# Order of casts, tiles and decay logs in the front of a hybrid attention block

## The chip, the core and the metric

One core of one Trainium2 chip runs the whole program. The metric is device time in microseconds (us), the median of several executions. The engines in the text: TensorE (PE, matmuls; PEld is its weight load), VectorE (DVE), ScalarE (ACT), GpSimd (POOL) and SyncE (SP, which here only issues DMAs). "PEq", "SPq" and the like are the engines' queues of issued work.

## What is computed

One layer of a streaming encoder for 512 frames of width 1024: RMSNorm, one wide projection `w_in`, three branches (gated linear attention, forgetting attention "Fox", cross attention into 256 memory tokens), their gated sum, an output projection, a squared-ReLU MLP and a last RMSNorm. What matters for the change:

```python
u = rmsnorm(h, g_mix[l])
proj = u @ w_in[l]
(gq, gk, gv, gg, ga, fq, fk, fv, ff, mq, gates) = split_cols(proj, PROJ_SIZES)

log_a = jax.nn.log_sigmoid(ga @ w_alpha_up[l] + b_alpha[l]) / GLA_TAU
...
log_f = jax.nn.log_sigmoid(ff + b_forget[l])
o_fox = forgetting_attention(fq, fk, fv, log_f)

mkv = rmsnorm(mem, g_mem[l]) @ w_mem_kv[l]
```

`ga` (16 columns) and `ff` (8 columns) are the low-rank input of the decay and the forget gate. Both go through a log-sigmoid: these are the decay logs. `rmsnorm(mem)` needs the sum of squares of each memory token.

## The kernel before

All matmul operands are kept as two parts, `hi` (the value cast to fp32r) and `lo` (the rest), and each product is three matmuls: hi by hi, hi by lo, lo by hi (`mm3`, L150 to L152). A weight chunk is 128 x 1024 (512 KB). It is loaded by SP into a ring of three buffers `raw` (or, for chunks 3, 4, 7 and 10 of the front, into a ring of two named `lead`), cast by ACT to `hi`, and subtracted by DVE to `lo`; `hi` and `lo` have rings of three. So a chunk's cast waits for its load and for the last matmul that read the buffer's older content, and a new load waits for the older chunk's subtraction.

Work on PE runs in the order in which the program traces it. On ACT, DVE, POOL and SP a planner orders instructions by a simulated time line: it takes what is ready in the simulation, earlier traced work first. Two things bind it. `in_order()` (L205) fixes the traced order on ACT, DVE and PE; the front stage from L348 on lies in it. `tc.issue_after(ins)` puts every instruction of its block that runs on the engine of `ins` behind `ins`.

The front: memory keys and values are projected from unnormalised memory tokens (chunks 0 to 7 of `FIRST_W`), while x is squared and its row scale is computed. The row scale is spread over partitions by eight small matmuls (`bcast_rows`, L241) and copied by ACT to `rxb` (L249). Then the eight tiles of x are handled one by one: `x_high(k)` (L412) scales tile k on DVE and casts it on ACT to `uhi`, `x_low(k)` (L416) subtracts on DVE to `ulo`. Between them stand the splits of weight chunks 7 (last memory values), the low-rank chunk (ACT cast L426, DVE subtraction L429), 9 (first Fox queries) and 10 (first Fox keys).

Behind it, the lead (L648 to L652): a low-rank projection (2 matmuls for each tile of x), the first pair's Fox queries (3 matmuls a tile) and keys (3 a tile) are traced as a staircase: low-rank tile s, queries tile s-1, keys tile s-2. `decay_logs()` (L478) multiplies the low-rank result by `wup` in four matmul pairs, each into its own PSUM bank, and takes Abs, Exp and Ln on ACT and minima and subtractions on DVE. The ring `pa` has four PSUM banks; the banks of the low-rank result, of the keys and of the four products follow each other in it. `fv = v_chunks(...)` is the projection of Fox's values: four chunks of eight units of three matmuls; a unit's number in `islice(fv, n)` counts such triples. `decay_sums()` (L490) multiplies the logs by triangular matrices, `decay_rows()` (L504) transposes the sums and writes them to DRAM. `mem_split()` (L627) squares the memory tokens (eight squares on ACT, seven adds on DVE into `memsum`), sums over partitions on PE (L231), and later scales and splits the memory's keys and values; its first part ends at `yield`.

In the profile L201 and L202 are the two halves of the helper `split`, L141 and L142 those of `split_w`, L297 and L303 those of `first_high` and `first_low`, L413 the scaling of x and L417 its low half, L463 and L464 the low-rank matmuls, L481 the four matmul pairs of the logs, L635 and L636 the squares and adds of the memory.

Of the kernel before, what the change touches and what calls it, by code (L numbers as in the profile page):

```python
# [13 lines left out]
AF = mybir.ActivationFunctionType  # L14
ALU = mybir.AluOpType
# [46 lines left out]
def hybrid_block(ctx, tc, chunks, wst, xT, memT, xN, cols, gffn, gfin, wup, cst, out):  # L62
# [214 lines left out]
    with pool("front") as fp:  # L277
        rxb = sg[3]
        xr = fp.tile([P, KT, S], F32, name="xr")
        FIRST_W = [chunks[j] for j in range(8)] + [("G",), ("T", "w_in", OFF["fq"]), ("T", "w_in", OFF["fk"])]  # L280
        raws, ready, loads = {}, {}, {}

        def first_load(i, n=1):
            late = i in (3, 4, 7, 10)
            raws[i] = (fp if late else wp).tile([P, 1024], F32, tag="lead" if late else "raw", name=nm("raw"),
                                                bufs=2 if late else 3)
            for j in range(n):
                sl = slice(j * 1024 // n, (j + 1) * 1024 // n)
                loads[i] = (nc.scalar if n > 1 and j < 3 else nc.sync).dma_start(raws[i][:, sl], wst[index[FIRST_W[i]]][:, sl]).ins
                if n > 1:  # L290
                    yield

        def first_high(i, n=1, j=0):
            if i not in ready:
                ready[i] = [wp.tile([P, 1024], F32R, tag=g, name=nm(g)) for g in ("hi", "lo")]
            sl = slice(j * 1024 // n, (j + 1) * 1024 // n)
            cast = nc.scalar.copy(ready[i][0][:, sl], raws[i][:, sl])  # L297
            if i > 4:
                next_sum(cast.ins)

        def first_low(i, n=1, j=0):
            sl = slice(j * 1024 // n, (j + 1) * 1024 // n)
            nc.vector.tensor_tensor(ready[i][1][:, sl], raws[i][:, sl], f(ready[i][0][:, sl]), op=ALU.subtract)  # L303

        def first_split(i, n=1, j=0):
            first_high(i, n, j)
            first_low(i, n, j)

        def first_w(i):
            run(first_load(i))  # L310
            first_split(i)

        get_plain = get_w

        def get_first(key):
            return ready[FIRST_W.index(key)]

        get_w = get_first
        mxh = fp.tile([P, KT, M], F32R, name="mxh")
        mxl = fp.tile([P, KT, M], F32R, name="mxl")  # L320
        xacc = dct[:, :S]
        warm = fp.tile([P, 1], F32, name="warm")
        nc.vector.memset(warm, 0.0)
        wz = fp.tile([P, 512], BF16, name="wz")
        nc.gpsimd.memset(wz, 0.0)
        ps = at_()
        for _ in range(12):
            nc.tensor.matmul(ps, wz[:, :P], wz, start=True, stop=True)

        kv = {}  # L330

        def mem_in(k):
            return sg[k // 2][:, k % 2 * M:k % 2 * M + M] if k < 6 else dct[:, 4 * S + (k - 6) * M:4 * S + (k - 5) * M]

        def mk_raw(h):
            return gkT[h // 2][:, (h % 2) * M:(h % 2) * M + M]

        def mk_proj(h):
            return gT(("T", "w_mem_kv", P * h), mxh, mxl, lambda ps: kv.update({h: ps}), n=M)

        def mk_take(h):
            nc.scalar.copy(mk_raw(h), kv[h][:, :M])

        def x_squares(*ks):
            for k in ks:
                sq_col(fp, xr, S, k, xacc, "x")

        with in_order():  # L348
            nc.scalar.activation(warm, warm, AF.Exp)
            nc.scalar.dma_start(cols_s, cols)  # L350
            quarters = first_load(0, 4)
            for j in range(4):
                to = sg[j] if j < 3 else dct[:, 4 * S:5 * S]
                nc.sync.dma_start(to.rearrange("p (k t) -> p k t", k=2), memT[:, 2 * j:2 * j + 2])
                next(quarters)

            def x_load(j):
                nc.sync.dma_start(xr[:, 2 * j:2 * j + 2], xT[:, 2 * j:2 * j + 2])

            run(first_load(1), first_load(2))  # L360
            x_load(0)
            run(first_load(3))
            for j in range(1, 4):
                x_load(j)
            nc.sync.dma_start(cst_s[:, :2 * P], cst[:, :2 * P])
            nc.sync.dma_start(cst_s[:, 5 * P:], cst[:, 5 * P:])
            run(first_load(4))
            for k in range(KT):
                m = mem_in(k)
                nc.scalar.mul(mxh[:, k, :], m, gmem[:, k:k + 1])  # L370
                nc.vector.scalar_tensor_tensor(mxl[:, k, :], m, gmem[:, k:k + 1], f(mxh[:, k, :]),
                                               op0=ALU.mult, op1=ALU.subtract)
                if k % 2 == 0:
                    first_split(0, 4, k // 2)
            first_split(1, 2, 0)
            first_split(1, 2, 1)
            first_split(2)
            x_squares(0, 1)
            run(mk_proj(0))
            first_split(3)  # L380
            x_squares(2, 3)
            run(mk_proj(1))
            x_squares(4, 5, 6, 7)
            run(mk_proj(2))
            mk_take(0)
            mk_take(1)
            first_split(4)
            run(mk_proj(3))
            rx = rms_cols(fp, xacc, S)
            first_w(5)  # L390
            mk_take(2)
            mk_take(3)
            mv = gN([("N", "w_mem_kv", 2 * j, 512) for j in range(4)], of(mxh, mxl), 2, mmt,
                    lambda t, ps: kv.update({("v", t): ps}))
            for i in (6, 7):
                run(first_load(i))
            g_raw = load_w(("G",))
            for i in (9, 10):
                run(first_load(i))
            run(islice(mv, 6))  # L400
            put = bcast_rows(fp, rx, S, rxb)
            next(put)
            first_high(6)
            run(put)
            first_low(6)
            run(islice(mv, 6))
            with tc.issue_after(loads[7]):
                nc.sync.dma_start(cst_s[:, 2 * P:5 * P], cst[:, 2 * P:5 * P])
                nc.sync.dma_start(wup_s, wup)
            ends = {}  # L410

            def x_high(k):  # L412
                nc.vector.scalar_tensor_tensor(xr[:, k, :], xr[:, k, :], gmix[:, k:k + 1], rxb, op0=ALU.mult, op1=ALU.mult)  # L413
                ends[0] = nc.scalar.copy(uhi[:, k, :], xr[:, k, :]).ins

            def x_low(k):  # L416
                ends[1] = nc.vector.tensor_tensor(ulo[:, k, :], xr[:, k, :], f(uhi[:, k, :]), op=ALU.subtract).ins  # L417

            x_high(0)
            x_high(1)  # L420
            first_split(7)
            run(mv)
            x_low(0)
            x_high(2)
            raw3, w3 = (t.rearrange("p (k c) -> p k c", k=KT) for t in (g_raw, both))
            nc.scalar.copy(both, g_raw)  # L426
            x_low(1)
            low = slice(64, P)
            nc.vector.tensor_tensor(w3[:, :, low], raw3[:, :, low], f(w3[:, :, low]), op=ALU.subtract)  # L429
            first_split(9)  # L430
            x_high(3)
            x_low(2)
            first_split(10)
            for k in range(4, KT):
                x_high(k)
                x_low(k - 1)
            x_low(KT - 1)
            for t in range(2):
                nc.scalar.copy(gqT[t], kv["v", t])
        u_ends = ends[0], ends[1]  # L440
        get_w = get_plain
# [15 lines left out]
    with pool("fox") as xp:  # L457
# [20 lines left out]
        def decay_logs():  # L478
# [4 lines left out]
                nc.vector.tensor_scalar(la[:, t, :], z[:, :256], 0.0, None, op0=ALU.min)  # L483
                nc.vector.tensor_scalar(lf[:, t, :], z[:, 256:], 0.0, None, op0=ALU.min)
            nc.scalar.activation(ab, ab, AF.Exp, scale=-1.0)
            nc.scalar.activation(ab, ab, AF.Ln, bias=1.0)
            nc.vector.tensor_tensor(lf, lf, ab[:, :, 256:], op=ALU.subtract)
            nc.vector.tensor_tensor(la, la, ab[:, :, :256], op=ALU.subtract)

        def decay_sums():  # L490
            ps = at_()
# [154 lines left out]
                split(mvh[:, t, :], mvl[:, t, :], gqT[t])  # L646

        lead = [low_rank(), *fox_pair(0)]  # L648
        for s in range(KT + 2):
            for i, g in enumerate(lead):  # L650
                if 0 <= s - i < KT:
                    next(g)  # L652
        with tc.issue_after(u_ends[0]), tc.issue_after(u_ends[1]):
            run(*lead)
            decay_logs()
            fv = v_chunks(OFF["fv"], v_evac)
            run(islice(fv, 14))
            nc.vector.tensor_copy(msk_s, cst_s[:, 5 * P:5 * P + 64])
        decay_sums()
        run(islice(fv, 2))  # L660
        decay_rows()
        mem = mem_split()
        next(mem)
        run(fv)
        run(fox_pair(1))
        run(mem)
# [922 lines left out]
```

## Time and profile before

| | us |
|---|---|
| runs, median of 3 (lowest, highest) | 816.41 (816.37, 817.52) |
| the profiled execution | 814.75 |
| its span in the profile | 813.0 |
| TensorE busy | 797.1 |
| VectorE busy | 574.7 |
| ScalarE busy | 457.6 |

The page gives busy times and shares of the span, the chain that ended last, and groups of instructions by line. The timeline of an engine gives for each entry its start and its duration in us, engine and line, the operation, the tile written and the tiles read, the shapes, and in brackets the idle time of the engine just before it and what ended that. Entries with a count merge equal neighbours, the duration is then that of all. The list of waits sums such idle times by waiter and releaser. The mean granted TensorE clock was 0.998 of full speed.

### The profile page before, as it was taken

What the parts mean: (1) busy time and instruction counts of PE and PEld (TensorE: products, weight loads), DVE (VectorE), ACT (ScalarE), POOL (GpSimd) and SP (SyncE); (2) the same over time, 40 slices, a digit from 0 to 9 for tenths busy, and PEclk for the clock granted to TensorE, in tenths of its full rate; (3) what the DMA queues carried; (4) which work ended last, traced back from release to release, by engine and by line L of the source; (5) the groups of instructions that cost most, each with busy time, mean ns of one, the idle gap of its engine ahead of it and who ended that gap; (6) DMA issues with size and microseconds to landing.
All of it is one profiled execution on the core that took longest, in us unless ns stands there. A gap on an engine that the chain in (4) does not pass through costs nothing.

```text
span 813.0 us, 12080 instructions
## 1 busy us (share of the span) xinstructions
PE 797.1 (98%) x4617; PEld 679.4 (84%) x4617; DVE 574.7 (71%) x877; ACT 457.6 (56%) x727; POOL 103.4 (13%) x124
## 2 busy tenths in 40 slices
PE   9889999999999999999999999999999999999995
PEld 6668887777888888888888889988998899889984
DVE  6673664464565489595969748895788678878896
ACT  7574645443553456454645636774676377537764
POOL 0001222001001033111110000011001100100122
PEclk9999999999999999999999999999999999999999
DMA  9524977777767868789884605888658966896685
GB/s 336 208 78 162 252 229 209 194 226 214 225 208 207 244 166 197 185 207 231 199 199 134 258 27 190 251 180 218 225 171 191 233 208 166 195 259 185 155 151 147
DMA packets 41178, 161.01 MB, mean 198 GB/s; under 512 B 4968, under 2 KB 6048, under 8 KB 39072
## 3 DMA queue, kind: packets, MB, share of 16 engines
q0 software_dynamic: 11632, 60.56, 36.3%
q1 hardware_dynamic: 27504, 95.31, 33.6%
q10 hardware_dynamic: 1984, 4.37, 1.7%
q8 instruction: 36, 0.59, 0.3%
q14 instruction: 22, 0.18, 0.1%
HBM read 156.26 MB, written 31.49 MB: 231 GB/s over the span
## 4 chain that ended last, share of the span: by engine, by line
PE 92%; DVE 3%; ACT 2%; DMA 1%; issue 1%; SPq 0%; POOLq 0%; DVEq 0%; ACTq 0%
PE mm L150 19%; PE mm L151 19%; PE mm L152 19%; PE a L150 4%; PE a L151 4%; PE a L152 4%; PE mm L1016 3%; PE mm L1017 3%; PE mm L1018 3%; PE a L1016 2%; PE a L1017 2%; PE a L1018 2%; PE mm L1389 1%; PE a L614 1%; DMA raw<-in_wst_dram 1%
## 5 line engine op out<-in xcount | busy, mean ns | idle before, releaser
L201 ACT CAST hi<-raw 128x1024 fp32r<-128x1024 f32 x77 | 80.9, 1051 | 62.6 <-PE mm L151 32.6
L202 DVE TENSOR_TENSOR lo<-raw,hi 128x1024 fp32r<-128x1024 f32 x77 | 94.1, 1222 | 30.3 <-ACT hi L201 30.3
L142 DVE TENSOR_TENSOR wlo<-raw,whi 128x1024 fp32r<-128x1024 f32 x44 | 55.9, 1272 | 63.4 <-ACT whi L141 59.1
L141 ACT CAST whi<-raw 128x1024 fp32r<-128x1024 f32 x44 | 46.2, 1051 | 82.8 <-issue 27.5
L152 PE MATMUL mm<-u2h,lo 128*128 128x256 f32 x224 | 63.4, 283 | 0.0
L151 PE MATMUL mm<-u2l,hi 128*128 128x256 f32 x224 | 63.4, 283 | 0.0
L150 PE MATMUL mm<-u2h,hi 128*128 128x256 f32 x224 | 63.4, 283 | 0.0
L1301 POOL DMA_DIRECT2D Y<-in_wst_dram x32 | 27.3, 854 | 262.6 <-DVE lo L202 185.8
L201 ACT CAST hi<-Y 128x1024 fp32r<-128x1024 f32 x34 | 35.6, 1048 | 32.5 <-PE mm L152 22.0
L202 DVE TENSOR_TENSOR lo<-Y,hi 128x1024 fp32r<-128x1024 f32 x34 | 41.6, 1223 | 17.4 <-ACT hi L201 17.4
L150 PE MATMUL mm<-hi,ch 128*128 128x512 f32 x128 | 49.8, 389 | 0.0
L151 PE MATMUL mm<-lo,ch 128*128 128x512 f32 x128 | 49.8, 389 | 0.0
L152 PE MATMUL mm<-hi,cl 128*128 128x512 f32 x128 | 49.8, 389 | 0.0
L201 ACT CAST hi<-g 128x1024 fp32r<-128x1024 f32 x30 | 31.6, 1054 | 30.4 <-PE a L1018 13.5
L202 DVE TENSOR_TENSOR lo<-g,hi 128x1024 fp32r<-128x1024 f32 x30 | 36.6, 1219 | 16.7 <-ACT hi L201 16.6
L150 PE MATMUL mm<-u2sh,hi 128*128 128x256 f32 x168 | 47.5, 283 | 0.0
L151 PE MATMUL mm<-u2sl,hi 128*128 128x256 f32 x168 | 47.5, 283 | 0.0
L152 PE MATMUL mm<-u2sh,lo 128*128 128x256 f32 x168 | 47.5, 283 | 0.0
L150 PE MATMUL mm<-uhi,whi 128*128 128x512 f32 x112 | 44.5, 397 | 0.0
L152 PE MATMUL mm<-uhi,wlo 128*128 128x512 f32 x112 | 43.7, 390 | 0.0
L151 PE MATMUL mm<-ulo,whi 128*128 128x512 f32 x112 | 43.6, 389 | 0.0
L150 PEld LDWEIGHTS mm<-u2h,hi 128*128 128x128 f32 x224 | 43.0, 192 | 0.2
(446 smaller groups left out, 2326.2 us busy)
## 6 DMA issues: line engine op xcount, KB each, us to landing
raw<-in_wst_dram SPq DMA_DIRECT2D x109, 512.0 KB, 5.4
Y<-in_wst_dram POOLq DMA_DIRECT2D x32, 512.0 KB, 5.4
raw<-T SPq DMA_DIRECT2D x28, 512.0 KB, 3.4
T<-in_wst_dram POOLq DMA_DIRECT2D x12, 1024.0 KB, 8.6
g<-in_wst_dram POOLq DMA_DIRECT2D x24, 512.0 KB, 5.8
Y<-in_wst_dram SPq DMA_DIRECT2D x16, 512.0 KB, 6.9
g<-in_wst_dram SPq DMA_DIRECT2D x12, 512.0 KB, 3.3
nFb<-dF ACTq DMA_DIRECT2D x8, 448.0 KB
```

Of the source, the lines that this page charges most:

```text
L141: cast = nc.scalar.copy(hi, raw)
L142: nc.vector.tensor_tensor(lo, raw, f(hi), op=ALU.subtract)
L150: nc.tensor.matmul(ps, lh, rh, start=start, stop=False)
L151: nc.tensor.matmul(ps, lh, rl, start=False, stop=False)
L152: nc.tensor.matmul(ps, ll, rh, start=False, stop=stop)
L201: nc.scalar.copy(hi, src)
L202: return nc.vector.tensor_tensor(lo, src, f(hi), op=ALU.subtract).ins
L614: nc.tensor.matmul(po[half[e], kt * P:], V[:, kt, 2 * j + e, :], PT[e][:, c0:c0 + S - kt * P], start=kt == 0, stop=kt == 3, skip_group_che ...
L1016: nc.tensor.matmul(ps[t], a, wh[:, kk, :], start=go, stop=False, **w)
L1017: nc.tensor.matmul(ps[t], a, wl[:, kk, :], start=False, stop=False, **w)
L1018: nc.tensor.matmul(ps[t], b, wh[:, kk, :], start=False, stop=k == 3, **w)
L1301: nc.gpsimd.dma_start(to, x, accum_op=ALU.add)
```

## The change

Four things are done. In the front, the cast of chunk 7 is traced ahead of the copy of the row scale, its subtraction stays behind the scaling of tiles 0 and 1 of x. The low-rank chunk's cast and subtraction and the cast of chunk 9 come ahead of tile 2 of x; the subtraction of chunk 9 comes behind the low half of tile 1. The lead no longer goes as a staircase: two tiles of low-rank, two of queries, low-rank 2, queries 2, three tiles of keys, and from tile 3 on low-rank, queries, keys of each tile in turn. `decay_logs()` is traced behind the first four units of Fox's values instead of ahead of them, and the first part of `mem_split()` must follow the logs' Ln on ACT and the last subtraction of the logs on DVE.

```diff
--- before.py
+++ after.py
@@ -401,6 +401,7 @@
             put = bcast_rows(fp, rx, S, rxb)
             next(put)
             first_high(6)
+            first_high(7)
             run(put)
             first_low(6)
             run(islice(mv, 6))
@@ -418,16 +419,17 @@
 
             x_high(0)
             x_high(1)
-            first_split(7)
+            first_low(7)
             run(mv)
             x_low(0)
-            x_high(2)
             raw3, w3 = (t.rearrange("p (k c) -> p k c", k=KT) for t in (g_raw, both))
             nc.scalar.copy(both, g_raw)
-            x_low(1)
             low = slice(64, P)
             nc.vector.tensor_tensor(w3[:, :, low], raw3[:, :, low], f(w3[:, :, low]), op=ALU.subtract)
-            first_split(9)
+            first_high(9)
+            x_high(2)
+            x_low(1)
+            first_low(9)
             x_high(3)
             x_low(2)
             first_split(10)
@@ -483,9 +485,9 @@
                 nc.vector.tensor_scalar(la[:, t, :], z[:, :256], 0.0, None, op0=ALU.min)
                 nc.vector.tensor_scalar(lf[:, t, :], z[:, 256:], 0.0, None, op0=ALU.min)
             nc.scalar.activation(ab, ab, AF.Exp, scale=-1.0)
-            nc.scalar.activation(ab, ab, AF.Ln, bias=1.0)
+            ln = nc.scalar.activation(ab, ab, AF.Ln, bias=1.0).ins
             nc.vector.tensor_tensor(lf, lf, ab[:, :, 256:], op=ALU.subtract)
-            nc.vector.tensor_tensor(la, la, ab[:, :, :256], op=ALU.subtract)
+            return ln, nc.vector.tensor_tensor(la, la, ab[:, :, :256], op=ALU.subtract).ins
 
         def decay_sums():
             ps = at_()
@@ -646,21 +648,21 @@
                 split(mvh[:, t, :], mvl[:, t, :], gqT[t])
 
         lead = [low_rank(), *fox_pair(0)]
-        for s in range(KT + 2):
-            for i, g in enumerate(lead):
-                if 0 <= s - i < KT:
-                    next(g)
+        for i in (0, 0, 1, 1, 0, 1, 2, 2, 2) + (0, 1, 2) * (KT - 3):
+            next(lead[i])
         with tc.issue_after(u_ends[0]), tc.issue_after(u_ends[1]):
             run(*lead)
-            decay_logs()
             fv = v_chunks(OFF["fv"], v_evac)
-            run(islice(fv, 14))
+            run(islice(fv, 4))
+            z_end = decay_logs()
+            run(islice(fv, 10))
             nc.vector.tensor_copy(msk_s, cst_s[:, 5 * P:5 * P + 64])
         decay_sums()
         run(islice(fv, 2))
         decay_rows()
         mem = mem_split()
-        next(mem)
+        with tc.issue_after(z_end[0]), tc.issue_after(z_end[1]):
+            next(mem)
         run(fv)
         run(fox_pair(1))
         run(mem)
```

## The prediction, made before the change was run

> **What bounds the kernel now.** I read the page first, then TensorE's list of waits, then the timelines of PE, ACT and DVE from 20 to 76 us, engine by engine.
>
> ```profile
> span 813.0 us, 12080 instructions
> PE 797.1 (98%) x4617; PEld 679.4 (84%) x4617; DVE 574.7 (71%) x877; ACT 457.6 (56%) x727; POOL 103.4 (13%) x124
> PE 92%; DVE 3%; ACT 2%; DMA 1%; issue 1%; SPq 0%; POOLq 0%; DVEq 0%; ACTq 0%
> ```
>
> PE is busy 98% of the span and is 92% of the chain that ended last. A change can save only where PE stands still or runs slow. The waits of PE over the whole span, longest first (waiter <- what released it: sum, times, longest):
>
> ```profile
> PE a L481 <- DVE K L202: 2.5, 1, 2.5
> PE a L328 <- POOL wz L325: 1.3, 1, 1.3
> PE a L464 <- DVE ulo L417: 1.1, 2, 0.5
> PE a L463 <- DVE both L429: 0.8, 1, 0.8
> PE mm L151 <- DVE lo L303: 0.7, 1, 0.7
> PE a L231 <- DVE dct L226: 0.6, 1, 0.6
> PE a L152 <- DVE lo L303: 0.5, 1, 0.5
> ```
>
> All seven end before 57 us, and the list names no wait after it. The second and sixth (the start, and the sum of x's squares near 20 us) stay as they are; the other five lie in the stretch that the diff touches. So the change is worth what it does to these five, less any new wait: past 57 us PE has no hole to give, only holes to gain.
>
> **The lead, 30.6 to 52.6 us.** PE's timeline (start, duration, operation; a matmul's duration overlaps the next one's):
>
> ```profile
> 30.62 0.40 PE L150 MATMUL mm<-hi,mxh 128*128 128x512 f32 x1
> 31.68 0.50 PE L151 MATMUL mm<-lo,mxh 128*128 128x512 f32 x1 [0.66 <-DVE lo L303]
> ...
> 47.12 0.39 PE L464 MATMUL a<-ulo,both 128*128 128x512 f32 x1
> ...
> 52.56 1.50 PE L481 MATMUL a<-wup_s,dct 128*128 128x264 f32 x6
> 56.54 0.71 PE L481 MATMUL a<-wup_s,dct 128*128 128x264 f32 x2 [2.48 <-DVE K L202]
> 56.89 0.59 PE L150 MATMUL mm<-whi,uhi 128*128 128x512 f32 x1
> ```
>
> From 47.12 to 52.56 there are 24 matmuls without a wait: 5.44 / 24 = 0.2267 us each. From 30.62 to 52.56 PE issues 12 matmuls of the last chunk of memory values, 16 of the low-rank projection, 24 of the first queries and 24 of the first keys: 76 x 0.2267 = 17.2 us. They took 21.94, so 4.7 us are waits and restarts. The causes stand on ACT and DVE:
>
> ```profile
> 26.73 0.59 ACT L249 COPY sg<-a 128x512 f32<-128x512 f32 x1 [1.13 <-PE a L247]
> 28.13 1.28 ACT L414 CAST uhi<-xr 128x512 fp32r<-128x512 f32 x2 [0.82 <-DVE xr L413]
> 29.32 1.04 ACT L297 CAST hi<-raw 128x1024 fp32r<-128x1024 f32 x1
> ```
>
> ```profile
> 27.35 1.41 DVE L413 SCALAR_TENSOR_TENSOR xr<-xr,cols_s,sg 128x512 f32<-128x512 f32 x2 [0.49 <-ACT sg L249]
> 30.40 1.23 DVE L303 TENSOR_TENSOR lo<-raw,hi 128x1024 fp32r<-128x1024 f32 x1 [1.64 <-ACT hi L297]
> ...
> 34.52 0.69 DVE L429 TENSOR_TENSOR both<-raw,both 128x512 fp32r<-128x512 f32 x1 [1.03 <-ACT both L426]
> ...
> 44.59 1.46 DVE L417 TENSOR_TENSOR ulo<-xr,uhi 128x512 fp32r<-128x512 f32 x2
> ```
>
> The cast of weight chunk 7 stands behind the casts of tiles 0 and 1 of x (29.32), so DVE stands idle 1.64 us ahead of its low half (30.40) and PE waits for that until 31.68. Everything behind it on DVE is late by the same.
>
> The change casts chunk 7 ahead of the copy of the row scale (26.73). It starts when ACT is free (26.73 less its idle 1.13: 25.6) and the load has landed. SP's queue shows chunk 7's load (16.08) right behind that of the low-rank chunk (14.80), of which the list of issues gives the landing (last number, us):
>
> ```profile
> 14.80 0.33 SPq L135 DMA_DIRECT2D raw<-in_wst_dram  x1
> 16.08 0.33 SPq L289 DMA_DIRECT2D raw<-in_wst_dram  x1
> raw<-in_wst_dram SPq DMA_DIRECT2D x1, 512.0 KB, 9.6
> ```
>
> The one landed at 24.4; with the same size and the same delay the other lands 1.3 us later, at 25.7, an estimate. So the cast runs 25.7 to 26.8, and the scale's copy slips from 26.73 to 26.8: 0.1 us. What stands behind it on ACT are the casts of x. A landing 1 us later would still be hidden, since DVE then reaches chunk 7's low half at 29.8 and ends it at 31.0, 0.1 us after PE wants it. Behind the scale, with the durations above (x scaled 0.7 a tile, its low half 0.68, a chunk's low half 1.2, the low-rank chunk's 0.69), DVE runs: x0, x1 to 28.8; chunk 7 to 30.0 (PE wants it at 30.85: no wait); x0 low 30.6; low-rank low half, whose cast ACT now ends at 30.4, to 31.2 instead of 35.2; x2 31.9; x1 low 32.5; queries' low half to 33.6; x3, x2 low to 34.9; one idle us for the keys' cast; keys' low half to 37.2; then two tiles of work of 1.3 us a tile, the last low half at 42.9 instead of 46.05.
>
> PE in the new order: memory values end at 33.3, low-rank 0, 1 to 34.2, queries 0, 1 to 35.6, low-rank 2 (x2 low at 34.9) to 36.1, queries 2 to 36.8, keys 0 from there, its third matmul at 37.2, on the edge of the keys' low half. After that each tile costs PE 8 x 0.2267 = 1.8 us and DVE 1.3. All waits go: **4.7 us saved** (4.4 at the other end, if the first queries and keys meet PE late by a restart each), the lead ends at 47.8. The low-rank row (35.27 in the list of waits as 0.8) goes for two reasons at once, its low half 4 us earlier and PE one wait earlier.
>
> Two loads of Fox's values reuse buffers that these splits free, so SP issues them 3 to 4 us earlier. Behind them SP holds only the next such loads, and the list of waits has no DMA in it: cost nothing, and nothing gained.
>
> **The logs, 52.6 to 56.9 us.** The last of the four decay matmul pairs (56.54) waits for the PSUM bank of the keys, whose evacuation (DVE K in the list of waits) is late: the memory's adds, the last at 55.47, and their squares stand around it.
>
> ```profile
> 58.82 1.28 ACT L486 ACT_TABLE_LOAD   x1
> 60.11 1.09 ACT L486 ACTIVATE dct<-dct 128x1056 f32<-128x1056 f32 x1
> ```
>
> ```profile
> 50.38 1.48 DVE L636 TENSOR_TENSOR memsum<-memsum 128x256 f32<-128x256 f32 x3 [1.02 <-ACT memsum L635]
> ...
> 55.47 0.42 DVE L636 TENSOR_TENSOR memsum<-memsum 128x256 f32<-128x256 f32 x1
> ...
> 61.34 1.22 DVE L488 TENSOR_TENSOR la<-la,dct 128x1024 f32<-128x1024 f32 x1
> ```
>
> Six matmuls of the logs take (1.50 - 0.39) / 5 = 0.22 us each, so the eight are worth 1.8 us; from 52.56 to 56.89 PE spent 4.3. **2.5 us are the wait.** In the new order PE has 12 matmuls of Fox's values (2.7 us) between the keys and the logs, and the 8 squares and 7 adds of the memory no longer stand in between on ACT and DVE. Keys end at 47.8. Even with two weight casts of 1.04 and their 1.23 subtractions ahead of it (low-rank bias, cast, queries, cast, keys), the keys' low half ends at about 52.5; with the priority of its place in the program at 50. The fourth pair is due at 47.8 + 0.2 + 2.7 + 6 x 0.22 = 52.0. I take no wait; the other end is 0.5. The four units need the first values' split: the cast can start when the last cast of x (about 42) and two copies are done, so it ends by 45.6, 2 us early.
>
> What the new order costs: one more change between kinds of matmul. The change at 56.89 took 0.43 to the next start instead of 0.23, so 0.2 to 0.3; I take **0.25**.
>
> **The squares behind the logs: the new wait.** The column sum of the squares (L231) is in PE's fixed order, and the second half of Fox's values is queued behind it.
>
> ```profile
> 67.22 0.17 DVE L497 COPY Fc<-a 128x8 f32<-128x8 f32 x1 [2.13 <-PE a L494]
> ...
> 68.59 0.50 PE L231 MATMUL a<-cst_s,memsum 128*128 128x1 f32 x4
> ```
>
> Today the sum is ready at 55.9 and wanted at 68.59: free. New: PE does the same work ahead of L231 and saves 4.7 + 2.5 - 0.25 = 6.95 on it, so L231 is due at 61.6. The fourth pair starts 4.5 us earlier than today (56.54 to 52.0), so Ln ends at 60.11 + 1.09 - 4.5 = 56.7 and the subtraction of the logs at 62.56 - 4.5 = 58.1. Only then may the adds start. With their squares they go at 1.48 / 3 = 0.49 each: 7 x 0.49 = 3.4, ready at 61.5. That is level with PE if nothing comes between. But the split of the fourth chunk of values becomes ready when PE is through with the first (55.4): a cast of 1.04 on ACT and 1.23 on DVE; and the eight short DVE steps of the decay sums (the first at 67.22 today, together about 1 us) come near 60. With both between the adds the sum is ready at about 63.7. So L231 waits between 0 and 2.1 us; I take a little under the middle, **0.9**, since the planner fills an engine's gaps with whatever is ready, and the adds leave gaps.
>
> Another doubt: up to here squares ran under the first table only, none behind Ln's load, and that load took 1.28 us (58.82). With a reload L231 would wait 1.3 us more, a rival below. [...]
>
> **Sum.** 4.7 + 2.5 - 0.25 - 0.9 = 6.05, about 6.1 us. Against the profiled execution's own 814.75 us (1.75 of it outside the span): 808.7. The three runs' median is 816.41, 1.66 above that execution, so **810.3**.
>
> **Rivals.**
> 1. Nothing comes between the adds, or the decay sums' chain is what PE meets first: 6.1 + 0.9 = 7.0 saved, 809.4. For it: 3.4 us of adds just fit. Against: the fourth chunk's split is ready inside that stretch.
> 2. The sum is later still: split and decay steps between (2.1) and a table reload (1.3), so L231 waits 3.4: 816.4 - 7.0 + 3.4 = 812.8. Against: behind Ln's load the trace has casts, copies and scaled copies, and no further load until the next Exp.
> 3. The other side. The planner keeps logs, squares and adds as one block ahead of the split of the values' second chunk, which PE wants at 52.5 + 0.2 + 2.7 = 55.4. If only the subtraction falls behind the adds, it ends at 61.5 + 1.2 = 62.7 and PE stands 7.3: 816.7. If the cast does too, with the reload, 61.5 + 1.3 + 1.05 + 1.23 = 65.1, PE stands 9.7: 816.4 - 7.0 + 9.7 = 819.1. It decides once that split ends after 62.4 (7.0 us of hold). Against: its buffer comes free with the last matmul of the queries at 47.6, nine us before the squares may start, and ACT and DVE have nothing else then but two evacuations and that split.
>
> [...]
>
> **Chances.** Forecast (L231 waits 0.3 to 1.7) 0.54, own range 809.8 to 811.2; rival 1 0.20; rival 2 0.10; rival 3 0.08 in its small form (within 0.2%) and 0.08 in its large one. So faster by over 0.2% (1.6 us; about what a measurement of this kernel can tell from no change) 0.84, same 0.08, slower 0.08. The range takes forecast and rivals 1 and 2, with up to 0.8 us for the spread of the runs: 808.6 to 813.3.
>
> **What would show it.** Right: no PE wait on lo, both or ulo between 30 and 48 us; the logs' eight matmuls without a hole, after twelve of Fox's values, ending near 52.5; PE's first wait past them at L231, about 1 us, released by DVE's memory adds. Wrong: the copy of the scale later than 27; a DVE wait for the keys' bank again; a wait on the values' wlo at 55; an ACT_TABLE_LOAD before the squares; or new waits of PE past 70 us, where the planner's order may also shift and today's list has none.

## The result, and the profile after

| | before | after |
|---|---|---|
| median of 6 runs, us (lowest, highest) | 816.44 (814.76, 817.52) | 809.34 (808.87, 811.03) |
| the profiled execution, us | 814.75 | 809.36 |
| its span, us | 813.0 | 807.6 |

The ratio of the times is 0.9917, 95% interval 0.9903 to 0.9930: 7.1 us faster by the medians, 5.4 us by the two profiled executions. The forecast was 810.3. Of the executions of the experiments below, one of e3 (1611.87 us) and one of e4 (2049.67 us) took about twice as long as the others or more, and the ratios leave these two out while the medians count them (without them 812.74 and 813.65).

First the page of the changed kernel: span, busy times, shares of the chain that ended last.

```profile
span 807.6 us, 12080 instructions
PE 795.8 (99%) x4617; PEld 679.5 (84%) x4617; DVE 574.9 (71%) x877; ACT 458.3 (57%) x727; POOL 107.2 (13%) x124
PE 93%; DVE 2%; DMA 1%; ACT 1%; issue 1%; SPq 0%; POOLq 0%; DVEq 0%; ACTq 0%
```

The busy times are those of before within 1.3 us on PE, ACT and DVE; the span is 5.4 shorter. So nothing was taken out of the work, holes were. PE's list of waits, over the whole span:

```profile
PE a L508 <- DVE Fc L502: 1.3, 1, 1.3
PE a L328 <- POOL wz L325: 1.3, 1, 1.3
PE a L231 <- DVE dct L226: 0.7, 1, 0.7
```

The five waits that the change aims at are gone, the two that it leaves alone are there, and one is new: the transpose of the decay sums (L508 here, L506 before) waits for the sums' last step on DVE. PE's timeline where the five stood:

```profile
33.42 0.39 PE L465 MATMUL a<-uhi,both 128*128 128x512 f32 x1
...
48.04 0.39 PE L150 MATMUL mm<-whi,uhi 128*128 128x512 f32 x1
...
50.77 2.10 PE L483 MATMUL a<-wup_s,dct 128*128 128x264 f32 x8
52.51 0.59 PE L150 MATMUL mm<-whi,uhi 128*128 128x512 f32 x1
...
61.12 0.40 PE L152 MATMUL mm<-whi,ulo 128*128 128x512 f32 x1
62.85 0.27 PE L508 MATMUL a<-cst_s,Fc 128*32 128x128 f32 x1 [1.33 <-DVE Fc L502]
62.96 0.50 PE L231 MATMUL a<-cst_s,memsum 128*128 128x1 f32 x4
```

The last memory values begin at 30.70 (30.62 before), Fox's values at 48.04: 17.34 us for the 76 matmuls that took 21.94. The eight matmuls of the logs follow each other (50.77 to 52.51, 1.74 us; 4.33 before). The sum of squares, L231, starts at 62.96 instead of 68.59: 5.6 us earlier, after a new loss of 1.5 (61.12 to 62.85 less one matmul). From there to PE's last matmul the two traces take 735.7 and 735.9 us.

ACT and DVE in the front show the moved casts:

```profile
25.02 1.98 ACT L297 CAST hi<-raw 128x1024 fp32r<-128x1024 f32 x2
26.91 0.57 ACT L249 COPY sg<-a 128x512 f32<-128x512 f32 x1
```

```profile
28.85 1.22 DVE L303 TENSOR_TENSOR lo<-raw,hi 128x1024 fp32r<-128x1024 f32 x1
29.98 0.69 DVE L418 TENSOR_TENSOR ulo<-xr,uhi 128x512 fp32r<-128x512 f32 x1
30.59 0.68 DVE L428 TENSOR_TENSOR both<-raw,both 128x512 fp32r<-128x512 f32 x1
...
41.58 1.46 DVE L418 TENSOR_TENSOR ulo<-xr,uhi 128x512 fp32r<-128x512 f32 x2
```

Two casts stand ahead of the copy of the row scale now, and it is 0.2 us late (26.91). DVE goes on without a hole up to the idle 1.04 us ahead of the keys' low half, which the prediction has: chunk 7's low half ends at 30.07, before PE asks for it at 30.92, and the last low half of x at 43.0 instead of 46.05.

DVE between the logs and the transpose:

```profile
56.96 1.22 DVE L490 TENSOR_TENSOR la<-la,dct 128x1024 f32<-128x1024 f32 x1
58.09 0.95 DVE L638 TENSOR_TENSOR memsum<-memsum 128x256 f32<-128x256 f32 x2
58.96 1.22 DVE L142 TENSOR_TENSOR wlo<-raw,whi 128x1024 fp32r<-128x1024 f32 x1
60.09 0.95 DVE L638 TENSOR_TENSOR memsum<-memsum 128x256 f32<-128x256 f32 x2
60.96 0.16 DVE L499 COPY Fc<-a 128x8 f32<-128x8 f32 x1
...
61.14 0.42 DVE L638 TENSOR_TENSOR memsum<-memsum 128x256 f32<-128x256 f32 x1
61.49 0.16 DVE L502 TENSOR_TENSOR Fc<-a,off 128x8 f32<-128x8 f32 x1
...
62.20 0.42 DVE L638 TENSOR_TENSOR memsum<-memsum 128x256 f32<-128x256 f32 x1
62.55 0.16 DVE L502 TENSOR_TENSOR Fc<-a,off 128x8 f32<-128x8 f32 x1
```

The adds start behind the subtraction of the logs, the split of the fourth values' chunk (L142) stands between them, and the steps of the decay sums (Fc; seven in this trace, where the prediction counts eight), which PE made ready at 60, start at 60.96 and take turns with the last three adds of 0.42. The last step ends at 62.7, the last add at 62.6.

### The profile page after: what moved, and what is told of

It is laid out like the page before. It is cut to its first block, busy times and chain, and to the rows that moved or that the text cites. A ratio compares the mean times of both kernels' runs of the same rounds, so it can differ in the third digit from the quotient of the medians.

```text
span 807.6 us, 12080 instructions
## 1 busy us (share of the span) xinstructions
PE 795.8 (99%) x4617; PEld 679.5 (84%) x4617; DVE 574.9 (71%) x877; ACT 458.3 (57%) x727; POOL 107.2 (13%) x124
## 4 chain that ended last, share of the span: by engine, by line
PE 93%; DVE 2%; DMA 1%; ACT 1%; issue 1%; SPq 0%; POOLq 0%; DVEq 0%; ACTq 0%
PE mm L150 20%; PE mm L151 19%; PE mm L152 19%; PE a L152 4%; PE a L150 4%; PE a L151 4%; PE mm L1020 3%; PE mm L1018 3%; PE mm L1019 3%; PE a L1018 2%; PE a L1020 2%; PE a L1019 2%; PE mm L1391 1%; PE a L616 1%; DMA raw<-in_wst_dram 1%
## 5 line engine op out<-in xcount | busy, mean ns | idle before, releaser
L202 DVE TENSOR_TENSOR lo<-raw,hi 128x1024 fp32r<-128x1024 f32 x77 | 94.2, 1223 | 29.9 <-ACT hi L201 29.9
L142 DVE TENSOR_TENSOR wlo<-raw,whi 128x1024 fp32r<-128x1024 f32 x44 | 56.7, 1291 | 63.9 <-ACT whi L141 56.8
L202 DVE TENSOR_TENSOR lo<-Y,hi 128x1024 fp32r<-128x1024 f32 x34 | 41.6, 1223 | 17.3 <-ACT hi L201 17.3
L202 DVE TENSOR_TENSOR lo<-g,hi 128x1024 fp32r<-128x1024 f32 x30 | 36.6, 1221 | 17.2 <-ACT hi L201 17.1
L151 PEld LDWEIGHTS mm<-u2l,hi 128*128 128x128 f32 x224 | 43.0, 192 | 0.2
```

The costliest lines, as they stand in the source:

```text
L142: nc.vector.tensor_tensor(lo, raw, f(hi), op=ALU.subtract)
L151: nc.tensor.matmul(ps, lh, rl, start=False, stop=False)
L202: return nc.vector.tensor_tensor(lo, src, f(hi), op=ALU.subtract).ins
```

## Experiments

Executions of one kernel differ by some tenths in when the same work comes: DVE's five scalings at L591 start between 100.52 and 100.81 us in the four profiles of the kernel before. So the table counts, in each profiled execution, from the first matmul of the last memory values to the first one behind the lead, and to L231; then the wait at the logs' fourth pair and at the transpose, as PE's waits give them, and the medians of 4 to 11 runs with the ratio to the kernel before on the same chip (whose median was 815.87 beside e1 to e4 and 816.38 beside e5 to e8).

| kernel | lead, us | to L231, us | fourth pair | transpose | median, us | ratio (95%) |
|---|---|---|---|---|---|---|
| before | 21.94 | 37.97 | 2.5 | 0 | 816.44 | |
| the change | 17.34 | 32.26 | 0 | 1.3 | 809.34 | 0.9917 (0.9903 to 0.9930) |
| e1 casts of the front alone | 18.74 | 36.38 | 2.5 | 0 | 813.31 | 0.9968 (0.9955 to 0.9982) |
| e2 lead's tile order alone | 20.44 | 38.86 | 3.2 | 0 | 815.98 | 1.0003 (0.9988 to 1.0018) |
| e3 both of these | 17.25 | 35.63 | 3.2 | 0 | 812.97 | 0.9965 (0.9952 to 0.9978) |
| e4 logs and gate alone | 21.90 | 36.66 | 0 | 1.3 | 813.69 | 0.9972 (0.9960 to 0.9983) |
| e5 gate alone | 21.90 | 37.33 | 1.8 | 0 | 814.35 | 0.9982 (0.9967 to 0.9997) |
| e6 logs alone | 21.88 | 35.20 | 0 | 0 | 812.68 | 0.9957 (0.9942 to 0.9972) |
| e7 change without gate | 17.37 | 31.44 | 0.5 | 0 | 808.40 | 0.9909 (0.9887 to 0.9931) |
| e8 change, rows later | 17.30 | 33.46 (12 matmuls more) | 0 | 0 | 807.71 | 0.9896 (0.9879 to 0.9913) |

**e1, e2, e3: which part of the front gives what.** e1 takes the first two hunks of the change (casts and subtractions), e2 the lead's new order, e3 both; logs and squares stay as before.

```diff
 e1, e3:
             first_high(6)
+            first_high(7)
             run(put)
...
-            first_split(7)
+            first_low(7)
...
+            first_high(9)
+            x_high(2)
+            x_low(1)
+            first_low(9)
 e2, e3:
+        for i in (0, 0, 1, 1, 0, 1, 2, 2, 2) + (0, 1, 2) * (KT - 3):
+            next(lead[i])
```

> Only the front's casts and subtractions in the new order; lead as a staircase, logs and squares as before. Theory A (both orders are needed): memory values and the low-rank tile 0 go without a wait, but the staircase asks for keys 0 and low-rank 3 at once, so PE still waits about 0.7 us for the keys' low half and 0.85 us for x3's low half: 3.0 of the lead's 4.7 us are saved, about 813.4 us (span 810). Theory B (the order of tiles alone makes the gain): under 1 us saved, 815.5 or more.

> Only the lead in the new order of tiles; front, logs and squares as before. Theory A: the waits for chunk 7's low half (0.8) and the low-rank low half (1.0) stay, the one for the keys' low half becomes 0.85, the others go: 1.6 us saved, about 814.8 us. Theory B: 4 us or more saved, 812.4 or less.

> Front and lead in the new order, logs directly behind the lead and squares ungated, as before. Theory A (the parts add up): 4.7 us saved and the wait for the keys' bank stays near 2.5 us: 811.7 us. Theory C (the parts overlap: with the lead 4.7 us earlier the keys' evacuation on DVE does not come earlier by as much, since squares and casts stand ahead of it): the wait grows to 4 us or more and only 2 to 3 us are saved, 813.5 to 814.5.

The lead shrinks by 3.2 us with the casts alone, by 1.5 with the tile order alone, by 4.7 with both: the two add up, as theory A says, and neither is enough. But little of it reaches the end of the kernel. With the lead earlier, the fourth pair of the logs waits 3.2 us instead of 2.5 in e2 and e3, since the keys' evacuation does not come earlier by the same. And behind the wait the matmuls of e1, e2 and e3 go at half speed for a while. The windows of e1 (PE busy, granted clock, DMA share, GB/s):

```profile
54.00:56.00 2.00, 2.00 (x7) 0.53 0.36 143
56.00:58.00 2.00, 2.00 (x7) 0.61 0.00 0
58.00:60.00 2.00, 2.00 (x11) 1.00 0.00 0
```

Seven matmuls in a window instead of ten or eleven, at a granted clock of 0.53 and 0.61, then full speed again. The two windows lack 0.94 and 0.78 us of clock: 1.7 us lost, which at half speed would be a stretch of 3.4 us, an estimate. e2's windows from 56 us (0.62, 0.52) and e3's from 52 us (0.59, 0.55) give the same 1.7. Up to L231, e1 keeps 1.6 of its 3.2 us, e2 loses 0.9 instead of gaining 1.5, and e3 keeps 2.3 of 4.7. So theory B falls. Theory C's mechanism shows in e2 and e3, the front passes part of its gain on to the next wait, but only 0.7 us of it: C expected a wait of 4 us or more, and most of what e3 loses is the clock, which no theory had. e1's median met the 813.4 that was expected, though by its profile it did so with an unforeseen loss of 1.6 us behind the hole, so it proves less than it seems; e2 and e3 missed what theory A gives them, by 1.2 and 1.3 us.

**e4, e5, e6: which part of the logs' move gives what.** All with the old front and lead. e4 has both parts, e5 only the gate on the squares, e6 only the logs behind four units of values.

```diff
 e4, e6:
             fv = v_chunks(OFF["fv"], v_evac)
-            run(islice(fv, 14))
+            run(islice(fv, 4))
+            decay_logs()
+            run(islice(fv, 10))
 e4, e5:
+        with tc.issue_after(z_end[0]), tc.issue_after(z_end[1]):
+            next(mem)
```

> Old front and lead; logs behind four units of the values, squares behind the logs. Theory A: 2.5 us of the keys' bank saved, 0.25 lost to a change of kind, and PE waits 1.3 to 1.5 us for the decay sums' last step at the transpose: 0.8 us net, 815.6 us. Theory C: the new wait at the transpose is smaller than 0.5 with the late front, 2 us saved or more.

> The kernel before, with the memory's squares and adds behind the logs, nothing else. If the squares and adds on ACT and DVE are what makes the keys' bank late, the wait of the logs' fourth pair falls from 2.5 us to under 1.3. If the two weight casts and their subtractions are, it stays above 2. Either way a new wait of 1 to 2 us comes at the transpose, so the net is -1 to +1.5 us: 815.5 to 818.

> The kernel before, with the logs behind four units of the values, squares not gated. If four units (2.7 us) of PE work alone cover the keys' evacuation, the wait of the fourth pair is under 0.5 us and no new wait comes at the transpose, since the squares are done early: 2.3 us saved, 814.1 us. If the squares keep the evacuation late, the wait stays at 1 us or more.

The wait at the keys' bank falls to 1.8 us with the gate alone and to nothing with the four units alone. So squares and adds are 0.6 us of the 2.5 (2.48 to 1.84), between the two cases of e5's expectation, under 1.3 or above 2. What is left in e5 shows on its DVE:

```profile
52.21 1.23 DVE L142 TENSOR_TENSOR wlo<-raw,whi 128x1024 fp32r<-128x1024 f32 x1 [3.78 <-ACT whi L141]
53.35 0.68 DVE L526 SCALAR_TENSOR_TENSOR Q<-mm,Q 128x512 fp32r<-128x512 f32 x1
53.95 1.22 DVE L142 TENSOR_TENSOR wlo<-raw,whi 128x1024 fp32r<-128x1024 f32 x1
55.08 0.69 DVE L202 TENSOR_TENSOR K<-a,K 128x512 fp32r<-128x512 f32 x1
```

Two subtractions of weights for Fox's values and the queries' low half go back to back ahead of the keys' low half, and the first of them waits for its cast. Work of PE put ahead of the logs covers all of it. The wait at the transpose shows in e4 and the changed kernel, where gate and move meet; it is in neither e5 nor e6. It takes both: with the gate alone, PE still has fourteen units between logs and sums instead of ten, and with the move alone, the squares are early. e5's expectation, a new wait either way and 815.5 us or more, was wrong for that reason: its median is 814.35. e4 saves 1.3 us to L231 (0.8 expected, and with the wait at the transpose that theory A has) and 1.45 between the profiled executions (814.75 to 813.30); the 2.2 by the medians meets theory C's number without its mechanism. e6 saves 2.8 to L231 and 3.7 by the medians (2.3 expected). In e6's profiled execution, the longest of its five, 1.6 of the 2.8 are lost again behind L231; 1.2 of these are PE's waits at the transposes of the first Fox pair, which the last section tells.

**e7, e8: the new wait.** e7 is the changed kernel without the gate; e8 keeps the gate and puts transpose and sum of squares four units later on PE.

```diff
 e7:
-        with tc.issue_after(z_end[0]), tc.issue_after(z_end[1]):
-            next(mem)
+        next(mem)
 e8:
-        run(islice(fv, 2))
+        run(islice(fv, 6))
         decay_rows()
```

> The changed kernel with the squares not gated. If the gate causes the wait at the transpose (its DVE steps interleave with the memory's adds), that wait goes; if the gate is what lets the keys' bank come free in time, a wait of about 1 us or more comes at the fourth pair. Theory A: the first without the second, span 806.1 to 806.4 against 807.6. Rival: the second, span 807.3 or more.

> The changed kernel with transpose and column sum of the squares four units (12 matmuls, 2.7 us) later on PE. If the wait at the transpose (1.3 us, 1.5 with the restart) is only DVE's steps being late against PE's place, it goes and nothing later waits: span 806.1, 807.9 us. If the rows that follow (write to DRAM, read back, mask, first scores) have no slack, the wait comes back at the first scores: span 807.6.

The first of PE's waits in e7, then all of e8's:

```profile
PE a L328 <- POOL wz L325: 1.3, 1, 1.3
PE a L483 <- DVE K L202: 0.5, 1, 0.5
...
```

```profile
PE a L328 <- POOL wz L325: 1.3, 1, 1.3
PE a L231 <- DVE dct L226: 0.4, 1, 0.4
```

Without the gate the transpose waits for nothing and the keys' bank costs 0.5 again: L231 comes 0.8 us earlier than in the changed kernel. By the profiles the gate is worth less than it costs here, so both the first and a small part of the rival's forecast came true, with the sum next to theory A's (span 806.5, where A said 806.1 to 806.4). By the medians this is not shown: the interval of e7's ratio holds the whole of the changed kernel's. e8 keeps both covers and has neither wait: its way to L231 less the 12 matmuls of 0.227 is 30.7 us, 1.5 less than in the changed kernel, and nothing later waits. The expected 807.9 was 807.71. It is the fastest kernel here: 8.5 us under the kernel before by its ratio, against 6.8 for the change by its own, though the two intervals overlap a little.

**e9 to e12: why the medians differ by more than the profiles.** The kernel before has two groups of times: of 15 runs in one session 9 lay between 814.6 and 815.1 and 6 between 816.2 and 817.8. Its profile is of the lower group, its median in the first six runs of the upper. e9 fills the hole ahead of the logs' fourth pair with ten matmuls whose result nobody reads; the other three are the kernel before, unchanged, for their profiles.

```diff
 e9:
                 z = at_()[:, :264]
+                if t == NT - 1:
+                    fill = mmt()
+                    for _ in range(10):
+                        nc.tensor.matmul(fill, uhi[:, 0, :P], uhi[:, 0, :], start=True, stop=True)
                 nc.tensor.matmul(z, gaT[:, t * P:(t + 1) * P], wup_s, start=True, stop=True)
```

> The kernel before with ten matmuls of 512 columns, whose result nobody reads, ahead of the logs' fourth pair: PE works through its 2.5 us hole instead of standing still. Ten times 0.227 is 2.3 us, so the path is as long as before. Theory H (in part of the executions the hole halves the granted clock for some 3.4 us behind it, which costs 1.6 us): the times fall into one group near 814.8 us and the group of the kernel before near 816.4 us is gone; median 814.5 to 815.2. Rival (the two groups of times come from elsewhere, such as the start): both groups stay, median 815.8 to 816.5.

> The kernel before once more, for its profile. Theory H: if the execution is near 816.4 us, the granted clock between 56 and 62 us is near 0.55 and matmuls there are 0.43 us apart; if it is near 814.8 us, the clock is 1.00 there. Rival: no relation.

> The same again: near 816.4 us with a low clock behind the hole, or near 814.8 us without one.

> The kernel before a third time. The one execution over 816 us that was profiled so far had no low clock behind the hole, but waits of 1.4 us at the first pair's transposes (near 104 us) and 0.9 us at the end. If this execution is over 816 us: the same waits again (theory W), or a low clock between 56 and 62 us (theory H). If it is near 814.8 us, neither.

e9: ratio 0.9996 (0.9986 to 1.0007), median 814.95 against 815.02; of its 11 runs one is over 816.2, against 6 of 15. That settles nothing: three more lie between, at 815.6 to 816.0, and the median that theory H asked for (814.5 to 815.2) is one that the kernel before had itself beside e9 (815.02). e10 (814.67) and e12 (814.60) are of the lower group and have a full clock behind the hole (1.00 in the windows from 56 to 62 us). e11 (817.04) is of the upper group and has a full clock there as well:

```profile
56.00:58.00 2.00, 1.42 (x6) 1.00 0.74 215
58.00:60.00 2.00, 2.00 (x10) 1.00 0.15 61
```

So theory H falls for this execution. Its 2.3 us stand elsewhere: 1.8 are three waits of PE that the profile of before does not have (PE's list in e11, in part):

```profile
PE mm L1389 <- DVE h L1182: 0.7, 1, 0.7
...
PE a L599 <- DVE P L591: 0.6, 1, 0.6
...
PE mm L599 <- DVE P L591: 0.5, 1, 0.5
```

Whether all executions of the upper group are of this kind stays open: one was profiled. The listed mean clock (0.996 for e11, 0.998 for e10 and e12) does not tell either: e11's clock is 1.00 in the windows up to 806 us (62 to 95 us are not among them) and low behind that, where PE ends, with 0.92 from 806 to 810 us and 0.50 from 810 to 815. That alone lowers the mean by 0.0035.

## Why the prediction was right, step by step

- **The lead, 4.7 us forecast, 4.6 measured** (21.94 to 17.34). The cast of chunk 7 went as reckoned: the copy of the scale is 0.2 us late instead of 0.1, and the cover holds with 0.85 us to spare. The last low half of x ends at 43.0 (42.9 forecast), the lead at 48.04 (47.8).
- **The logs, 2.5 us forecast, 2.6 measured** (4.33 to 1.74). The keys' low half on DVE (L202) ends at 52.1, between the 50 and the 52.5 of the prediction, and so just as the fourth pair wants it; e7 shows how thin that is, with 0.5 us of wait once the squares are back.

```profile
51.42 0.68 DVE L202 TENSOR_TENSOR K<-a,K 128x512 fp32r<-128x512 f32 x1
```

- **The change of kind, 0.25 forecast, nothing measured**: the values behind the keys start without a delay, and the delay of 0.2 behind the logs (52.51) is the one that before has at 56.89.
- **The new wait, 0.9 forecast, 1.5 measured**, within the 0 to 2.1 of the prediction. The mechanism was the one described: adds that start only behind the subtraction of the logs, the fourth chunk's split between them, the sums' steps in their way. But PE met it one instruction sooner than the prediction put it, at the transpose, and the sums' steps released it; a wait at L231 that the adds release, the sign that the prediction named, is not there. The last add ends at 62.6, so L231 would have waited about 1.2 us had the transpose been ready at 61.4. There is no table load ahead of the squares: they follow Ln at once.

```profile
55.73 1.09 ACT L488 ACTIVATE dct<-dct 128x1056 f32<-128x1056 f32 x1
56.72 0.40 ACT L634 ACTIVATE memsum<-sg 128x256 f32<-128x256 f32 x1
```

- **The sum**, 6.05 us, against 5.4 between the two profiled executions: 0.6 of the difference is the new wait, the change of kind gives 0.25 back, 0.1 goes before the lead and 0.2 past L231.
- **The step that failed** is the last one: "The three runs' median is 816.41, 1.66 above that execution" carried the 1.66 over to the changed kernel. It is no constant. The changed kernel's median (809.34) lies on its profiled execution (809.36); the 1.66 belonged to a second group of executions of the kernel before. Profile to profile the forecast was 808.7 and the measurement 809.36, too good by 0.7; the median came out 1.0 better than forecast, the two errors having opposite signs. So the median meets the range in part by luck: it lies below the forecast's own 809.8 to 811.2 and beside the 809.4 of rival 1. That rival's second condition (the sums' chain is what PE meets first) came true, but not its price of nothing: the traces show a wait of 1.5 us and 5.4 saved, not 7.0.
- Rival 3, values' second chunk behind the squares: not seen. Its cast ran before Ln, and PE has no wait on the values' weights.

## What to carry to other kernels

When PE is busy 98% of the span, add up its holes and ask of each what will be late next: the lead's reordering was worth 4.7 us in its own stage and 2.3 up to L231 when the logs' wait was left behind it (e3, 0.7 lost to a longer wait and 1.7 to the clock), and all of it when the two were done together. A wait can be covered by moving work of PE that is ready in front of it (in e6 2.5 us to nothing, in e8 1.3); before gating other engines' work, ask whether what the gate delays has slack: here it had none, and by the profiles the gate cost more than it saved (e7 is at L231 0.8 us sooner without it). And take a gain from two profiled executions of the same group of times, not from a median and an offset.

## What was not expected of the hardware

**A hole on PE cost more than its length.** In e1, e2 and e3 the granted clock was 0.52 to 0.62 in two neighbouring windows of 2 us behind a wait of 2.5 to 3.2 us, at a price of 1.7 us (half the clock for some 3.4 us, an estimate from these windows); in the four profiled executions of before, with the same wait of 2.5 us in the three whose waits are listed, the clock behind it was full (1.00 from 56 to 62 us). The changed kernel has e3's front without this hole (waits of 1.3 us at most), and its clock is 1.00 in every window up to 800 us. e7 and e8 have no such hole either: they take 31.44 and, without the 12 matmuls more, 30.7 us to L231, where the changed kernel without its wait of 1.5 takes 30.8, so a loss of 1.7 has no room there. So in these profiles the fall comes only with the hole, though not every hole brings it; what sets it off is not shown. Among ten runs each, two of e1 (811.4 and 811.8 us, the next 813.0) and two of e2 (814.2 and 814.4, the next 815.7) may have been spared; none of these was profiled.

**DVE and POOL were slow beside each other.** DVE's five scalings of Fox's P (L591) in before, and in e11 with POOL's mask adds beside them:

```profile
100.75 1.78 DVE L591 TENSOR_SCALAR P<-P,ri 128x256 f32<-128x256 f32 x5
...
103.15 2.89 POOL L548 TENSOR_TENSOR nFb<-nFb,cst_s 128x512 f32<-128x512 f32 x2 [7.20 <-DMA nFb<-dF]
```

```profile
100.52 1.46 POOL L548 TENSOR_TENSOR nFb<-nFb,cst_s 128x512 f32<-128x512 f32 x1 [7.02 <-DVE ri L590]
100.81 5.19 DVE L591 TENSOR_SCALAR P<-P,ri 128x256 f32<-128x256 f32 x5
102.59 1.33 POOL L548 TENSOR_TENSOR nFb<-nFb,cst_s 128x512 f32<-128x512 f32 x1 [0.61 <-DVE P L591]
```

A third mask follows (104.41, 1.29 us); the rows of five merge 256 to 512 columns. Where the masks come after the scalings, these five take 1.78 us (1.80 in e10). In e11 three masks run beside them and they take 5.19, in e6 two and they take 4.21, and PE then waits at the transposes of the first Fox pair (0.6 and 0.5 us in e11, 0.7 and 0.5 in e6). In the changed kernel, e7 and e12 a mask starts while the five run: there the five keep 1.79 to 1.80, and it is the masks that are long, 2.67 for the first in the changed kernel and 3.92, 4.38 and 3.97 for the first two together, where one alone takes 1.3. In e8 a mask of 1.29 runs beside the two scalings ahead of the five: those two take 1.37 instead of 0.53, and the five behind them 1.78. So either engine was the slower one at some time; why is not shown, and it was not tried by itself. In before, the masks started when the rows' DMA landed, so the landing may decide which of the two an execution gets; that stays open.
